# Moving the residual gates' sums, packing the keys' weights and taking turns with results in a two-layer attention trunk

## The chip, the cores and the metric

The kernel runs on one core of one Trainium2 chip. The metric is device time in microseconds of one execution. TensorE (PE) multiplies, VectorE (DVE), ScalarE (ACT) and GpSimd (POOL) work on tiles, and SyncE (SP) issues the transfers (DMAs). Each engine takes its own instructions strictly in order; between engines they wait on semaphores.

## The reference

Two layers of a trunk over 512 latent tokens (an 8 x 64 grid) and 256 context tokens, 1,024 channels. Each layer is one mixer with two branches that share an input projection:

```
mod = silu(c) @ w_ada + b_ada            # shift, scale, gate: 3 x 1024; for x and for ctx
h   = rmsnorm(x, norm_g) * (1 + scale) + shift
a_k, a_v, b_k, b_v, a_q, b_q, a_z, b_z, g_a, g_b = split(h @ w_in)
a   = neighbourhood attention(qknorm(a_q), qknorm(a_k), a_v) + all context keys    # 8 heads of 64
b   = grouped attention(rope(qknorm(b_q)), rope(qknorm(b_k)), b_v)                 # 8 query, 2 key heads
o   = sigmoid(g_a) * ((a * silu(a_z)) @ w_o_a) + sigmoid(g_b) * ((b * silu(b_z)) @ w_o_b)
x   = x + gate * (o @ w_out)
```

Layer 0 does this for the context too (which attends to the context alone); layer 1 updates the latent tokens only. The result is x. What the text calls the residual gate is the last third of `mod`.

## The kernel before

Tokens lie in tiles of 128: four latent, two of context. Activations are kept with channels on the partitions (`hx`, 8 blocks of 128 channels). Numbers are float32; each product of two matrices is made of three (`mm3`, lines 344 to 348): both sides are split into a high part (a cast on ACT) and a low part (a subtraction on DVE or POOL), and high x high, high x low and low x high are added up. A token projection of 512 columns (`tok_proj`, line 356) is thus 24 PE products of 128x512 for each token tile; a channel projection (`chan_proj`, line 363) is the same with the weights as the stationary side.

A layer goes through these stages: keys of branch A (`C_AK`, 512 columns), values of A (`C_AV`), queries of A (`C_AQ`), neighbourhood attention over 8 heads, keys and values of branch B (`C_BKV`, 256 columns), queries of B (`C_BQ`), grouped attention over 8 heads, the second output projection, and `w_out` with the residual. Inside the attention stages a list of pieces (`fill`: projections of the z paths and of the g gates, then `w_o_a`) is spread over the heads by `pipeline` (line 822), so that PE has products to do while softmax runs on the other engines. For head h, `scores_of(h)` makes four score tiles (PE), and for each the maximum (DVE), the exponential (ACT), the reciprocal and the scaling of the probabilities (DVE, or POOL for two of four). `values_of(h - 1)` transposes probabilities in groups of four 128x128 blocks (line 654), splits them (cast on ACT, line 657; subtraction on DVE, line 658) and multiplies them with the values.

Weights: `load_w` (line 308) loads one block of 128 channels at a time into one of three `raw` buffers, casts it on ACT into `whi` and subtracts into `wlo`; these are rings of 8 buffers in the pool `wp`, or, with `own`, rings of 8 in a pool of the stage. `load_w2` (line 323) loads two blocks of 256 columns into one 128x512 buffer and so does cast and subtraction for both at once. The queries of A and of B use `own`; the pool of B's stage (`bp`) reuses the memory of the neighbourhood attention's pool and can be written only when that memory comes free.

Sums for `mod`: `ada_steps` (line 200) yields steps. One loads a part of silu(c) to all partitions (`cb`); each of the others loads a 128x512 block of `w_ada` (`rawb`, two buffers, 256 KB) and makes a sum of products over its columns on DVE (line 222). The blocks 16 to 23 are those of the residual gate, two halves (h) each, and two vectors (latent and context) in layer 0, one in layer 1: 32 sums in layer 0, 16 in layer 1. They are made in grouped attention, `att["per"]` steps after each score tile (two in layer 0, one in layer 1), and are followed by `ada_gate`, which writes the gate to memory (`gd`) to be read before the residual. The blocks 0 to 15 of layer 1's `mod` are summed in layer 0: half 0 in the values' and queries' tiles of A, half 1 in the `w_out` stage.

Evacuation of key and query results: `head_rstd` (square on ACT, sum on DVE, two steps on POOL), multiply (DVE), for B the rotation (`rope_heads`, line 464: multiply with the cosines on DVE, with the sines on POOL, add on DVE), then transposes on PE. These are put off: `to_channels` appends them to `hp["late"]`, and `tok_proj` emits those that are more than `hp["lag"]` tiles old, chained to stand behind PE's last instruction (`after_products`, line 381). The lag is 2. In layer 0 the first projection is made for all six token tiles at once, in six PSUM banks, as the normalised input arrives; its six results are then evacuated one after the other (lines 595 to 600) before the values' tiles begin.

What is written in this order is then ordered by the framework, engine by engine, before the run: it places instructions by estimated times and by the emission order as priority. Buffers wait for their last reader.

Of the kernel before, what the change touches and what calls it, by code (L numbers as in the profile page):

```python
# [7 lines left out]
F32 = mybir.dt.float32  # L8
# [18 lines left out]
NP_GQ = (10, 10)  # L27
# [4 lines left out]
PRE_NA, PRE_GQ = 1, 2  # L32
XB, RX = 6, 2
# [14 lines left out]
def hybrid_kernel(es: ExitStack, tc, x, ctx, cvec, w_ada, w_ada0, small, gvec, w_in, w_o_a, w_o_b, w_out,  # L48
# [151 lines left out]
    def ada_steps(l, tiles, halves, nv, pool):  # L200
# [13 lines left out]
        def dot(h, i, v):  # L214
# [4 lines left out]
            ins = nc.cur_bb.bb.instructions  # L219
            before = next(j for j in reversed(ins) if j.engine == mybir.EngineType.DVE)  # L220
            n = len(ins)
            V.tensor_tensor_reduce(o, w, cb[h][:, v, :], 1.0, 0.0, ALU.mult, ALU.add, asum[:, i, h, v:v + 1])
            for j in nc.cur_bb.bb.instructions[n:]:
                if j.engine == mybir.EngineType.DVE:
                    tc.add_manual_dep(j, before.name, mybir.DependencyInfo(
                        mybir.DependencyClass.NoSync, mybir.DependencyReason.DATA), reason="program order")
# [81 lines left out]
    def load_w(src, col0, n, nk, lo_eng, k0=0, own=None):  # L308
# [3 lines left out]
        for k in range(k0, k0 + nk):  # L312
            raw = raw_tile()
            nc.sync.dma_start(raw[:, :n], src[128 * k:128 * k + 128, col0:col0 + n])
            hi = pool.tile([128, 512], F32R, tag="whi" + x, name=nm("whi"), bufs=8)
            S.copy(hi[:, :n], raw[:, :n])  # L316
            lo = pool.tile([128, 512], F32R, tag="wlo" + x, name=nm("wlo"), bufs=8)
# [63 lines left out]
    def after_products(fn):  # L381

        ins = nc.cur_bb.bb.instructions
        n, pe = len(ins), mybir.EngineType.PE
        last = next(i.name for i in ins[::-1] if i.engine == pe)
        fn()
        for i in nc.cur_bb.bb.instructions[n:]:
            if i.engine == pe:
# [4 lines left out]
    def turn_late(n):  # L393

        while len(hp["late"]) > n:
            after_products(hp["late"].pop(0))
# [67 lines left out]
    def rope_heads(npair, ps, rs, ta, tb, dst, t):  # L464
# [4 lines left out]
        r = hp["p"].tile([128, n], F32, tag=f"rr{npair}", name=nm("rr"), bufs=3)  # L469
# [11 lines left out]
    def layer(l, hx, nxt, mid):  # L481
# [5 lines left out]
        W = w_in[l]  # L487
        gq = gcol[:, 48 + 2 * l:49 + 2 * l]
# [93 lines left out]
        if first:  # L582
# [13 lines left out]
            for t in range(6):  # L596
                ev(t, pss[t])
            for fn in hp["late"]:
                fn()
            hp["late"] = []  # L600
            hp["lag"] = 2
            bg = ada_steps(1, range(16), (0,), 2, hp["p"])
        else:
            hp["p"] = bgp_es.enter_context(tc.tile_pool(name=f"cp{l}", bufs=1, reuse_waits="tile"))
            w = load_w(W, C_AK, 512, KT, mix_lo)
            for t in range(6):
                tok_proj(w, 512, a_hx, t, evac_na(kav, False, gk, 4))
            bg = []
# [3 lines left out]
        for t in range(6):  # L612
            tok_proj(w, 512, a_hx, t, evac_va(va))
            if t > 2:
# [20 lines left out]
        if True:  # L635
# [127 lines left out]
            def na_scores(h, q, kh, kl):  # L763
                load_bias(h)
                ps_ = []
                for i in range(4):
# [23 lines left out]
                    run(att["bg"], att["per"])  # L790
# [342 lines left out]
```

## Time and profile before

| | |
|---|---|
| median of three runs | 1167.61 us (1165.52 to 1169.21) |
| the profiled execution, its own time | 1166.55 us |
| its span, first to last instruction | 1164.8 us |
| mean granted clock of PE | 0.997 |
| PE busy | 1127.1 us of the span |
| DVE, ACT, POOL busy | 812.0, 574.3, 498.0 us |
| DMA | 134.05 MB, mean 115 GB/s |

Lines that begin with an engine, a line number and an operation are groups of instructions or single ones; out<-in are the program's tile names (`pst` the PSUM tile of transposes, `pss` of scores, `psv` of values, `psf` and `psx` of projections; `pth` and `ptl` the parts of the split probabilities; `rr` rotated keys or queries; `gah` and `gal` the gated result of branch A; `raw`, `whi`, `wlo` the weights; `rawb`, `cb` the operands of the sums for `mod`). The number in "L654" is the line of the kernel. PE's products overlap, and their ends are modelled, so a busy PE is not a PE at its peak; the time from one start to the next tells more. In a chain, "issue" is time in which an engine waited for nothing that the profile shows.

The stages by time, in us from the span's start: start-up and first projection to 75, values and queries of A to 150, neighbourhood attention to 310, keys and queries of B to 386, grouped attention to 565, closing projections to 700, and in layer 1 keys, values and queries of A to 782, neighbourhood attention to 897, keys and queries of B to 957, grouped attention to 1096, closing projections to the end.

### The profile page before, as it was taken

How to read it: one execution, taken by the hardware profiler on the slowest of the kernel's cores; microseconds unless marked ns; L12 is line 12 of the kernel's file. 1: busy time of each engine (PE TensorE's matmuls, PEld its weight loads, DVE VectorE, ACT ScalarE, POOL GpSimd, SP SyncE). 2: the span in 40 equal slices, each digit the busy share in tenths (PEclk: the TensorE clock that was granted, in tenths of full speed). 3: DMA queues.
4: the chain of work that ended last, by engine and by line, in shares of the span. 5: the costliest groups of instructions: out<-in, count | busy, mean ns of one | idle time of the engine just before them, and what ended most of it. 6: DMA issues, size and time to landing. Idle time of an engine off the chain costs nothing.

```text
span 1164.8 us, 17332 instructions
## 1 busy us (share of the span) xinstructions
PE 1127.1 (97%) x6078; PEld 948.9 (81%) x6078; DVE 812.0 (70%) x1512; ACT 574.3 (49%) x1175; POOL 498.0 (43%) x463
## 2 busy tenths in 40 slices
PE   5999999999999999999999999999999999999998
PEld 4688888988988888888788787888888878877686
DVE  4556588876364799798588755349877757898573
ACT  5452266665343555666431355337665445756531
POOL 3362354443275334353411227345544664645311
PEclk9999999999999999999999999999999999999999
DMA  9534212221351343461434423403322525452133
GB/s 372 200 110 136 71 46 65 84 83 63 111 164 47 115 134 100 81 259 37 139 133 123 151 71 92 126 25 107 104 74 66 171 90 182 142 176 91 37 132 95
DMA packets 88129, 134.05 MB, mean 115 GB/s; under 512 B 10757, under 2 KB 52713, under 8 KB 86377
## 3 DMA queue, kind: packets, MB, share of 16 engines
q1 hardware_dynamic: 88040, 132.94, 35.3%
q8 instruction: 48, 0.79, 0.3%
q14 instruction: 41, 0.33, 0.1%
HBM read 115.58 MB, written 17.32 MB: 114 GB/s over the span
## 4 chain that ended last, share of the span: by engine, by line
PE 72%; DVE 10%; POOL 6%; issue 4%; DMA 3%; ACT 2%; SPq 0%; ACTq 0%; POOLq 0%; DVEq 0%
PE psx L348 10%; PE psx L346 10%; PE psx L347 10%; PE psf L346 8%; PE psf L347 8%; PE psf L348 8%; PE pst L654 4%; PE pss L703 2%; PE pss L704 2%; PE pss L780 2%; POOL rsb L255 2%; DVE ptl L658 2%; DMA rawb<-in_w_ada_dram 1%; PE psv L948 1%; DVE mx L930 1%
## 5 line engine op out<-in xcount | busy, mean ns | idle before, releaser
L658 DVE TENSOR_TENSOR ptl<-pst,pth 128x512 fp32r<-128x512 f32 (+1 forms) x176 | 116.1, 671 | 41.0 <-ACT pth L657 40.0
L657 ACT CAST pth<-pst 128x512 fp32r<-128x512 f32 (+1 forms) x176 | 98.9, 576 | 91.7 <-PE pst L654 63.3
L346 PE MATMUL psf<-hx,whi 128*128 128x512 f32 (+1 forms) x368 | 139.4, 379 | 0.0
L347 PE MATMUL psf<-hx,whi 128*128 128x512 f32 (+1 forms) x368 | 138.3, 376 | 0.0
L348 PE MATMUL psf<-hx,wlo 128*128 128x512 f32 (+1 forms) x368 | 138.2, 375 | 0.0
L333 POOL TENSOR_TENSOR wlo<-raw,whi 128x512 fp32r<-128x512 f32 x64 | 91.0, 1425 | 109.9 <-ACT whi L331 96.5
L346 PE MATMUL psx<-whi,hx 128*128 128x512 f32 (+1 forms) x368 | 136.9, 373 | 0.0
L347 PE MATMUL psx<-wlo,hx 128*128 128x512 f32 (+1 forms) x368 | 136.2, 370 | 0.0
L348 PE MATMUL psx<-whi,hx 128*128 128x512 f32 (+1 forms) x368 | 133.8, 370 | 0.0
L319 POOL TENSOR_TENSOR wlo<-raw,whi 128x512 fp32r<-128x512 f32 (+1 forms) x52 | 67.4, 1296 | 149.6 <-ACT whi L316 132.0
L316 ACT CAST whi<-raw 128x512 fp32r<-128x512 f32 (+1 forms) x112 | 65.2, 592 | 112.6 <-PE psx L348 38.3
L331 ACT CAST whi<-raw 128x512 fp32r<-128x512 f32 x128 | 77.6, 621 | 53.2 <-DMA raw<-in_w_in_dram 39.6
L654 PE MATMUL pst<-ident,p 128*128 128x128 f32 x640 | 100.6, 273 | 1.7 <-DVE ptl L658 1.2
L654 PEld LDWEIGHTS pst<-ident,p 128*128 128x128 f32 x640 | 78.1, 141 | 13.7 <-DVE ptl L658 1.0
L644 POOL TENSOR_TENSOR p<-p,r 128x512 f32<-128x512 f32 (+1 forms) x64 | 85.7, 1339 | 5.2
L333 DVE TENSOR_TENSOR wlo<-raw,whi 128x512 fp32r<-128x512 f32 x64 | 62.7, 980 | 31.0 <-ACT whi L331 30.6
L319 DVE TENSOR_TENSOR wlo<-raw,whi 128x512 fp32r<-128x512 f32 (+1 forms) x60 | 48.2, 807 | 45.9 <-ACT whi L316 45.6
L643 POOL TENSOR_SCALAR r<-r 128x1 f32<-128x1 f32 x64 | 21.5, 336 | 137.1 <-DVE r L638 126.6
L346 PEld LDWEIGHTS psx<-whi,hx 128*128 128x128 f32 x368 | 69.8, 190 | 11.9 <-issue 0.8
L348 PEld LDWEIGHTS psf<-hx,wlo 128*128 128x128 f32 x368 | 69.4, 189 | 11.9
L348 PEld LDWEIGHTS psx<-whi,hx 128*128 128x128 f32 x368 | 69.6, 189 | 11.3
L346 PEld LDWEIGHTS psf<-hx,whi 128*128 128x128 f32 x368 | 69.5, 189 | 11.1 <-ACT zt L502 0.3
(239 smaller groups left out, 3065.8 us busy)
## 6 DMA issues: line engine op xcount, KB each, us to landing
raw<-in_w_in_dram SPq DMA_DIRECT2D x160, 256.0 KB, 2.9
rawb<-in_w_ada_dram SPq DMA_DIRECT2D x64, 256.0 KB, 2.7
gs<-zt SPq DMA_DIRECT2D x32, 256.0 KB, 2.4
raw<-in_w_out_dram SPq DMA_DIRECT2D x32, 256.0 KB, 2.8
tg<-gs SPq DMA_DIRECT2D x4, 1536.0 KB, 8.6
rawx<-in_w_ada_dram SPq DMA_DIRECT2D x4, 1024.0 KB, 6.4
rawy<-in_w_ada_dram SPq DMA_DIRECT2D x4, 1024.0 KB, 12.2
raw<-in_w_o_a_dram SPq DMA_DIRECT2D x16, 256.0 KB, 3.3
```

Source lines behind the costliest of these rows:

```text
L255: G.tensor_tensor(b[:, :w], a[:, :w], ehalf[:, :w], ALU.pow)
L316: S.copy(hi[:, :n], raw[:, :n])
L319: e.tensor_tensor(lo[:, :n], raw[:, :n], F(hi[:, :n]), ALU.subtract)
L331: S.copy(hi, raw)
L333: lo_eng(i).tensor_tensor(lo, raw, F(hi), ALU.subtract)
L346: T.matmul(ps, lhs[0], rhs[0], start=first, stop=False)
L347: T.matmul(ps, lhs[0], rhs[1], start=False, stop=False)
L348: T.matmul(ps, lhs[1], rhs[0], start=False, stop=last)
L644: G.tensor_tensor(p[:, c0:c1], p[:, c0:c1], r[:, i:i + 1].to_broadcast([128, c1 - c0]), ALU.mult)
L654: T.transpose(pt[:, c0:c0 + 128], src, ident)
L657: S.copy(hi[:, n0:n1], pt[:, n0:n1])
L658: V.tensor_tensor(lo[:, n0:n1], pt[:, n0:n1], F(hi[:, n0:n1]), ALU.subtract)
```

## The change

1. The residual gate's sums are yielded by `gate_steps(halves, pool)`. Layer 0 makes half 0 in the neighbourhood attention, one step after each score tile from head 4 on, and half 1 (followed by `ada_gate`) in grouped attention, one step after each score tile. Layer 1 makes both halves in the values' and queries' tiles of A, and none in grouped attention. Grouped attention of layer 1 has 11 buffers for probabilities instead of 10.
2. The weights of B's keys and values are loaded with `load_w2`. Those of B's queries are loaded before the keys' products, the first four blocks into `wp`, the other four into a ring of four in the stage's pool.
3. During B's keys the lag is 3 instead of 2, with a fourth buffer for rotated keys. The cosine and sine tables for the queries are made after the third key tile; before, they were made with those for the keys, ahead of all.
4. In layer 0, five results of the first projection are evacuated before the values' tiles, the sixth after the first of them; their transposes are put off with a lag of 4 that goes down to 2.

```diff
-NP_GQ = (10, 10)
+NP_GQ = (10, 11)
...
-    def load_w(src, col0, n, nk, lo_eng, k0=0, own=None):
+    def load_w(src, col0, n, nk, lo_eng, k0=0, own=None, bufs=8):
...
-        r = hp["p"].tile([128, n], F32, tag=f"rr{npair}", name=nm("rr"), bufs=3)
+        r = hp["p"].tile([128, n], F32, tag=f"rr{npair}", name=nm("rr"), bufs=4 if npair == 1 else 3)
...
+        nv = 2 if first else 1
+
+        def gate_steps(halves, pool):
+            return (ada_steps(l, range(16, 24), halves, nv, pool)
+                    + ([lambda: ada_gate(l, nv)] if 1 in halves else []))
...
-            for t in range(6):
+            for t in range(5):
                 ev(t, pss[t])
-            for fn in hp["late"]:
-                fn()
-            hp["late"] = []
-            hp["lag"] = 2
+            hp["lag"] = 4
             bg = ada_steps(1, range(16), (0,), 2, hp["p"])
         else:
...
-            bg = []
+            bg = gate_steps((0, 1), hp["p"])
+            run(bg, 1)
...
         for t in range(6):
             tok_proj(w, 512, a_hx, t, evac_va(va))
+            if first:
+                if t == 0:
+                    ev(5, pss[5])
+                hp["lag"] = max(2, hp["lag"] - (t > 0))
             if t > 2:
                 run(bg, per_bg)
...
-                    run(att["bg"], att["per"])
+                    run(att["bg"], 1)
...
-                att["bg"], att["per"] = bg, -(-len(bg) // 30)
                 prev = None
                 for h in range(8):
+                    att["bg"] = bg if h > 3 or pm["n"] == 1 else []
...
-            pipeline(fill, 9, na_first, values_of(za, na_values))
+            bg = gate_steps((0,), att["p"]) if first else []
+            pipeline(fill, 9, na_first, values_of(za, na_values), bg=bg)
...
-            cosn = hp["p"].tile([128, 512], F32, tag="sq", name=nm("cosn"), bufs=2)
+            cosn = hp["p"].tile([128, 512], F32, tag="cosn", name=nm("cosn"), bufs=1)
...
-            for i in range(2):
+
+            def make_tabs(i):
                 for j in range(2):
                     V.tensor_tensor(tabs[:, i, j], cosn[:, j],
                                     gbc[:, i, :].unsqueeze(1).to_broadcast([128, 4, 64]), ALU.mult)
+            make_tabs(1)
...
-            w = load_w(W, C_BKV, 256, KT, mix_lo)
+            bg = []
+            w = load_w2(W, C_BKV, KT, mix_lo)
+            w_q = load_w(W, C_BQ, 512, 4, bq_lo) + load_w(W, C_BQ, 512, 4, bq_lo, 4, hp["p"], 4)
+            hp["lag"] = 3
             for t in range(6):
                 tok_proj(w, 256, a_hx, t, evac_bkv)
+                if t == 2:
+                    behind(ON_DVE, lambda: make_tabs(0))
+                run(bg, 1)
+            hp["lag"] = 2
             qbv = big("qb").rearrange("p (j n) -> p j n", j=4)
-            w = load_w(W, C_BQ, 512, KT, bq_lo, own=hp["p"])
...
-            nv = 2 if first else 1
-            bg = ada_steps(l, range(16, 24), (0, 1), nv, att["p"]) + [lambda: ada_gate(l, nv)]
-            run(bg, 1)
+            bg = gate_steps((1,), att["p"]) if first else []
             pipeline(fill, 8, gq_first, values_of(zb, gq_values), early, bg)
```

`behind(engine, fn)` is `after_products` with the engine as a parameter; the sums use it with DVE, as they did before with the same code in place.

More of the change, by code (lines that the diff above doesn't have):

```diff
@@ L218, in dot @@
             o = w if v == nv - 1 else pool.tile([128, 512], BF16, tag="junk", name=nm("junk"), bufs=1)
[L219 to L226, printed above, removed]
+            behind(ON_DVE, lambda: V.tensor_tensor_reduce(o, w, cb[h][:, v, :], 1.0, 0.0, ALU.mult, ALU.add,
+                                                          asum[:, i, h, v:v + 1]))
         res = []
@@ L379, in hybrid_kernel, with behind @@
     hp = {"late": [], "lag": 0}
[L381 removed]
+    def behind(engine, fn):
         ins = nc.cur_bb.bb.instructions
[L384 to L385 removed]
+        n = len(ins)
+        last = next(i.name for i in ins[::-1] if i.engine == engine)
         fn()
         for i in nc.cur_bb.bb.instructions[n:]:
[L388 removed]
+            if i.engine == engine:
                 tc.add_manual_dep(i, last, mybir.DependencyInfo(
@@ L395, in turn_late @@
         while len(hp["late"]) > n:
-            after_products(hp["late"].pop(0))
+            behind(ON_PE, hp["late"].pop(0))
     def run(fill, n):
```

11 lines of the change are left out of this document (7 added, 4 removed).

## The prediction

> **What bounds the kernel now.** I read the page's busy shares first, then TensorE's (PE's) waits, then busy time by stage, then the chain and the timelines where PE stands still.
>
> ```profile
> PE 1127.1 (97%) x6078; PEld 948.9 (81%) x6078; DVE 812.0 (70%) x1512; ACT 574.3 (49%) x1175; POOL 498.0 (43%) x463
> ```
>
> PE is the bound: the sum of its idle is 38 us, and no edit here removes a product or a transpose (both built programs hold equally many). So the change can only win or lose PE's standing time. A busy share hides some of it, because ends are modelled; I therefore took PE's starts from the timeline. In dense stretches a 128x512 product starts 0.230 us after the one before, a 128x256 one 0.119, a transpose 0.108; what a step takes beyond this is loss. That gives 51 us in all: 14.6 before 70 us (start-up, not touched), 1.2 in 150 to 310 (layer 0's neighbourhood attention), 1.7 in 310 to 386 (its keys and queries of branch B), 4.3 in 386 to 475 and 4.0 in 475 to 565 (its grouped attention), 0.3 in 712 to 782 (layer 1's values and queries of A), 4.8 in 782 to 897 (layer 1's neighbourhood attention), 4.6 in 897 to 957, 2.3 in 957 to 1060, 8.8 in 1060 to 1096 (layer 1's branch B: projections, grouped attention, its end). Between 70 and 150 it is zero.
>
> ```profile
> PE pst L422 <- DVE rr L477: 4.1, 7, 1.4
> PE psv L948 <- DVE ptl L658: 2.0, 7, 0.5
> ```
>
> Outside start-up the named waits are those two: transposes of rotated keys or queries (L422), and value products behind the split in DVE (L658). By stage (columns: stretch, length, then PE, weight load, DVE, ACT, POOL busy):
>
> ```profile
> 220.00:310.00 90.00, 90.00 (x572) 80.68 (x571) 55.76 (x114) 48.81 (x112) 31.96 (x36) 1.00 0.19 63
> 385.00:475.00 90.00, 88.03 (x519) 75.98 (x517) 82.49 (x161) 49.23 (x107) 31.85 (x28) 1.00 0.36 115
> ...
> 712.00:782.00 70.00, 69.64 (x323) 57.21 (x323) 27.99 (x40) 28.34 (x48) 33.31 (x29) 1.00 0.28 84
> ...
> 957.00:1060.00 103.00, 101.63 (x520) 84.61 (x519) 85.04 (x153) 62.82 (x121) 50.80 (x43) 1.00 0.52 166
> 1060.00:1096.00 36.00, 32.16 (x172) 23.50 (x171) 27.54 (x46) 22.50 (x44) 16.78 (x16) 1.00 0.11 36
> ```
>
> DVE is at 92% where grouped attention carries the gate sums (L222) in layer 0 and at 83% in layer 1, but at 62% and 40% in the two stretches to which they go.
>
> **The change part by part**, against the profiled execution's 1166.55 us (span 1164.8); the median of the runs, 1167.61, is 1.1 above it.
>
> *Gate sums moved.* Layer 0 keeps 16 of its 32 sums in grouped attention, one step per score tile instead of two; 16 go to heads 4 to 7 of neighbourhood attention. All 16 of layer 1 go to its values' and queries' tiles.
>
> ```profile
> L222 DVE CUSTOM_DVE_ANT_0 rawb<-rawb,cb x64: 667/691/1889, 92.5 to 1030.4; 128x512 f32<-128x512 f32 x64
> ```
>
> In 385 to 475 its 32 sums took 27.7 us, 0.87 each; 16 fewer free 13.9 us of 82.5, so DVE falls to about 76%. Stretches at such a load lose little: 150 to 220, with DVE at 88% (61.3 of 70), lost 0.5. I take 1.7 of the 4.3 back; ends 0 (the losses are latencies) and 3.5. The 4.0 after 475 lies in a part whose order on PE is unchanged: 0.
>
> In layer 1 two of the last sums stand just ahead of a stall of 1.1 us:
>
> ```profile
> 1017.52 1.78 DVE L222 CUSTOM_DVE_ANT_0 rawb<-rawb,cb 128x512 f32<-128x512 f32 x1
> ...
> 1019.31 1.70 DVE L222 CUSTOM_DVE_ANT_0 rawb<-rawb,cb 128x512 f32<-128x512 f32 x1
> ```
> ```profile
> 1023.55 0.50 PE L703 MATMUL pss<-gk,qs 128*128 128x512 f32 x1 [0.91 <-ACT p L932]
> ```
>
> Two sums, 3.5 us, delay maximum and exponential, and the score product behind them waits. Gone: 1.5 of the 2.3 (ends 0 and 2.0). The 16 sums there take 14.7 us; with them gone, and an eleventh buffer for probabilities, the built order puts scores ahead. After the last output-projection piece of `w_o_a` that can fill a gap, the old order has 6 score tiles and 22 groups of four transposes left, the new one 1 and 16. In this end PE loses 8.8 us in 22 groups, 0.4 each. Six groups fewer are 2.4 us. One stall of 1.4 us (1078.4) comes from two exponentials of 0.90 on ACT ahead of a cast that PE needs; with five score tiles gone I take 1.1 of it. Sum 3.5; ends 0 (the groups meet a busy DVE elsewhere) and 6.
>
> What they cost where they go. Neighbourhood attention, layer 0: 55.8 us of DVE plus 16 at 0.87, 14, are 70 of 90, 78%; the stretch at 88% lost 0.5 in 70 us, so 0.6; I take 1.0, with -0.3 and +3.8 (the 385 to 475 rate, 4.3 in 90) as ends. Layer 1's values and queries: 28 plus 14 are 42 of 70. Its 16 weight loads (256 KB, 2.7 us to landing) and two vector loads now stand on SP's queue, and the write of the gate ahead of the first bias load; a load waits for the sum two before it, so SP can stand for a tile (5.5 us) before the next weights. Layer 0 does the same from 92 to 134 with 32 sums, and PE lost nothing there. 0.5; ends 0 and 3.
>
> A sum's cost is not one number: 97 of 112 took 0.69 us on average, 15 took 1.59, and POOL ran during 24% of the short ones' time, 80% of the long ones'. The Trainium skill (SBUF — State Buffer, Who interferes with whom) has the rule: a DVE instruction with two SBUF inputs contends with a GpSimd one that reads SBUF, and the later of the two is blocked; these rows agree, and it speaks against putting sums beside POOL's work.
>
> *Keys' weights packed, queries' weights earlier.* Eight loads, casts and splits of 128x256 become four of 128x512, in both layers; the casts are then 4 x 0.62 us. Half the queries' weights move ahead of the keys' products, into the slots that this frees; four, not eight, still wait for attention's memory to come free. That is the cause of layer 1's queue:
>
> ```profile
> 918.03 4.69 DMA raw<-in_w_in_dram
> ...
> 922.75 0.62 ACT whi L331
> ...
> 926.11 1.68 POOL rsb L255
> ...
> 949.49 1.76 DVE rr L477
> ```
>
> The first query tile ends on PE at 917.9, but ACT stands at weight casts until 923.9 before it squares it, so its transposes come to PE 1.4 us late (932.5), and the ones after it queue on POOL. In the new order one cast stands there, not two after a 2.5 us wait. From 918 the chain (square 0.6, sum 0.7, POOL 2.3, multiplies 1.4, POOL 1.3, add 0.7, issue) ends near 926.5, PE wants it at 931.
>
> *Rotated keys later.* A lag of three tiles gives one 2.9 us tile more before a key's transpose; the tables for queries (one pair of multiplies, 0.75 us) leave the start of the stage. Together I take back 3.7 of 4.6 in layer 1 (ends 0 and 4.4) and 0.8 of 1.7 in layer 0 (0 and 1.5). Price: the second weight chunk of the gates now needs the slots that the queries hold, so two casts and two POOL splits (1.3 each) stand among the last query tiles' chains; the new order also puts layer 1's third query transposes 33 products after the second ones instead of 20, 3.0 us more cover.
>
> *First projection.* Five results are copied at once and the sixth after the values' first tile, transposes spread over six tiles. PE lost nothing between 70 and 150, with DVE at 65%: 0, and the cover is six result banks; if it fails, one copy (0.7) shows.
>
> Sum: -1.7 -1.5 -3.5 +1.0 +0.5 -3.7 -0.8 = -9.7, so 1156.9; I say 1157.
>
> **Rivals.**
> *The end of layer 1 stays latency-bound.* For it: after 1080.7 no maximum and no exponential is left there, and PE still loses 4.1 us in eleven groups. Then the 3.5 stay: 1160.4.
> *Shared reads.* If all moved sums meet POOL, each takes 1.59: neighbourhood attention has 81 of 90 us on DVE and pays 3.8 instead of 1.0: 1159.7. Against it: POOL is busy 36% there, 35% where they came from. The page above would make it so only where POOL's reads come first.
> *The change moves the stalls.* The orders are fixed ahead of time; stalls freed in one place may reappear at the next instruction in line, as 4.8 us in layer 1's neighbourhood attention and 4.0 after 475 are untouched. Then some 2 us net remain: 1164.5.
> *Slower: the shared weight slots.* ACT is in order. If a cast of the second gate chunk waits for the queries' last tile, all behind it (square, copies of transposes) waits, and PE at those transposes. One tile of products, 5.5 us, in each layer, with the 4.5 of this stage not won: 1156.9 + 4.5 + 11 = 1172.4. It decides from about 4 us a layer on. Against: slots come free one by one as the last tile passes them, the first 0.7 us after it starts.
>
> **How the numbers follow.** Forecast 0.45 (own range 1152 to 1161), end latency 0.18, shared reads 0.12, moved stalls 0.13, slots 0.12. About 0.3% (3.5 us) is what a measurement of this kernel can tell from no change. The first three are faster, 0.75; moved stalls 0.13 is the same; slots 0.12 is slower. The range runs from 1151 (the good ends of half the terms) to 1167, leaving out most of the slots' case and little below.
>
> **What would show it.** Right: DVE near 78% in layer 0's grouped attention up to 475; no 1.4 us wait of L422's transposes in layer 1; the square of the first query tile within 1 us of its product; less than 5.5 us lost in the last 36 us before the closing projections. Wrong: PE waits inside layer 0's heads 4 to 7 for maxima; SP standing at gate loads while a weight is due; ACT standing at a weight cast among the query tiles.

## The result, and the profile after

| | before | after |
|---|---|---|
| median, us | 1166.57 (4 runs, 1165.51 to 1169.21) | 1156.08 (4 runs, 1154.84 to 1156.70) |
| profiled execution, its span | 1166.55, 1164.8 | 1154.84, 1153.1 |
| PE's mean granted clock | 0.997 | 0.998 |

The ratio is 0.9905, with an interval of 0.9885 to 0.9926: faster by 10.5 us. The forecast was 1157, from the likeliest case and the sum of its seven terms. The profiled execution of the changed kernel is the fastest of its four, 1.2 us under their median; the traces therefore differ by a little more than the medians do.

The page of the changed kernel, busy times and the chain that ended last by engine:

```profile
PE 1123.5 (97%) x6078; PEld 949.3 (82%) x6078; DVE 811.9 (70%) x1508; ACT 573.2 (50%) x1167; POOL 494.5 (43%) x459
...
PE 83%; DVE 7%; issue 3%; POOL 2%; ACT 2%; DMA 1%; ACTq 0%; POOLq 0%; DVEq 0%
```

The other engines' busy times are as before within 1%, as are the counts on PE. What differs is where the work stands: in the profile before, the same row of the chain began `PE 72%; DVE 10%; POOL 6%`. The chain that ended last now lies on PE for 83% of the span. PE's busy share, 97% in both, says nothing of this.

PE's waits in the last 36 us before the closing projections changed, and so did those in layer 1's keys and queries of B. After, from 940 to 1090 us (waiting instruction, what it waited for, us in total, times, longest):

```profile
PE psv L961 <- DVE ptl L661: 1.8, 2, 1.5
PE pst L657 <- DVE ptl L661: 0.9, 2, 0.4
```

The wait of the transposes (line 422 before, 417 after) for rotated keys and queries, 4.1 us before and the longest outside start-up, has no row at all now. The value products are still the ones that wait for the split in DVE.

Busy time by stretch, after (length, then PE, weight load, DVE, ACT, POOL): layer 0's neighbourhood attention from 219, its grouped attention from 386, layer 1's values and queries of A, its grouped attention, and its end.

```profile
219.00:311.00 92.00, 91.65 (x585) 82.08 (x585) 69.89 (x149) 50.27 (x113) 38.83 (x36) 1.00 0.29 88
386.00:475.00 89.00, 88.11 (x534) 77.40 (x533) 68.55 (x130) 50.29 (x107) 30.62 (x28) 1.00 0.28 87
711.00:781.00 70.00, 70.00 (x324) 57.74 (x324) 38.73 (x73) 27.41 (x47) 33.31 (x27) 1.00 0.52 142
...
949.00:1060.00 111.00, 110.70 (x576) 92.41 (x575) 89.08 (x137) 71.34 (x138) 52.33 (x48) 1.00 0.33 110
1060.00:1084.00 24.00, 21.23 (x114) 15.33 (x112) 16.23 (x24) 14.07 (x27) 11.87 (x11) 1.00 0.13 46
```

DVE fell to 77% where half of the sums left (386 to 475), rose to 76% and 55% where they went, and the end is 24 us long, not 36.

To compare kernels I took PE's loss in each stage as the prediction did: the time from one PE start to the next beyond 0.230, 0.119 and 0.108 us. Stages are bounded here by events, the first and last product of their kind, and not by the clock, so that a shift doesn't move work between them; "GQ" is grouped attention, "NA" neighbourhood attention, "w" the last piece of the output projection `w_o_a` that can fill a gap. One profiled execution each, us:

| stage | before | after | sums alone | weights alone | lag undone |
|---|---|---|---|---|---|
| start-up, A's projections, layer 0 | 14.3 | 14.6 | 15.0 | 15.0 | 14.4 |
| NA, layer 0 | 1.2 | 1.7 | 1.6 | 1.2 | 1.6 |
| B's keys and queries, layer 0 | 1.7 | 0.5 | 2.3 | 0.7 | 0.2 |
| GQ, layer 0, to the first `w_o_a` piece | 5.5 | 3.1 | 3.2 | 4.7 | 3.2 |
| GQ, layer 0, rest | 4.1 | 4.4 | 4.0 | 4.4 | 4.4 |
| closing, layer 0 | 2.2 | 1.4 | 2.1 | 1.4 | 2.0 |
| A's projections, layer 1 | 0.8 | 0.5 | 0.5 | 0.8 | 0.5 |
| NA, layer 1 | 4.8 | 4.8 | 4.8 | 4.8 | 4.9 |
| B's keys and queries, layer 1 | 4.6 | 0.2 | 4.1 | 0.1 | 0.9 |
| GQ, layer 1, to w | 2.3 | 1.6 | 1.7 | 2.4 | 1.5 |
| GQ, layer 1, its end | 8.7 | 6.1 | 6.1 | 8.7 | 6.0 |

The differences between before and after (with -0.8 in both for the closing part of layer 1) add up to -11.6 before rounding, -11.3 by the table's rounded figures; the spans differ by 11.7. So the whole gain is PE's standing time, in four places: the projections of B in both layers, the first part of layer 0's grouped attention, and the end of layer 1's. The first row runs from 13.8 to 18.0 and "closing, layer 0" from 1.3 to 2.2 over the kernels below without order by their edits; what changes only there I don't read. A stage that two kernels have alike loses the same in both: neighbourhood attention of layer 1 loses 4.8 or 4.9 in all twelve kernels, here and below, that leave it as it is, and the end is the same within 0.1 us in the five that have the sums moved and nothing else changed there, and in the five that have it as before.

### The profile page after: what moved, and what is told of

The parts are those of the page before. It is cut to its first block, busy times and chain, and to the rows that moved or that the text cites. A ratio compares the mean times of both kernels' runs of the same rounds, so it can differ in the third digit from the quotient of the medians.

```text
span 1153.1 us, 17284 instructions
## 1 busy us (share of the span) xinstructions
PE 1123.5 (97%) x6078; PEld 949.3 (82%) x6078; DVE 811.9 (70%) x1508; ACT 573.2 (50%) x1167; POOL 494.5 (43%) x459
## 4 chain that ended last, share of the span: by engine, by line
PE 83%; DVE 7%; issue 3%; POOL 2%; ACT 2%; DMA 1%; ACTq 0%; POOLq 0%; DVEq 0%
PE psx L341 12%; PE psx L343 12%; PE psx L342 12%; PE psf L341 9%; PE psf L342 9%; PE psf L343 9%; PE pst L657 4%; PE pss L706 2%; PE pss L707 2%; PE psv L961 2%; PE pss L783 1%; PE psv L960 1%; PE pst L417 1%; DVE wlo L328 1%; DVE ptl L661 1%
## 5 line engine op out<-in xcount | busy, mean ns | idle before, releaser
L661 DVE TENSOR_TENSOR ptl<-pst,pth 128x512 fp32r<-128x512 f32 (+1 forms) x176 | 116.0, 672 | 46.4 <-ACT pth L660 45.4
L328 POOL TENSOR_TENSOR wlo<-raw,whi 128x512 fp32r<-128x512 f32 x68 | 95.5, 1408 | 107.2 <-ACT whi L326 86.2
L314 POOL TENSOR_TENSOR wlo<-raw,whi 128x512 fp32r<-128x512 f32 x44 | 61.4, 1397 | 140.4 <-ACT whi L311 123.8
L326 ACT CAST whi<-raw 128x512 fp32r<-128x512 f32 x136 | 82.4, 621 | 55.6 <-DMA raw<-in_w_in_dram 39.6
L311 ACT CAST whi<-raw 128x512 fp32r<-128x512 f32 x96 | 58.7, 623 | 102.1 <-PE psx L343 38.6
L657 PE MATMUL pst<-ident,p 128*128 128x128 f32 x640 | 99.9, 272 | 1.4 <-DVE ptl L661 0.9
L328 DVE TENSOR_TENSOR wlo<-raw,whi 128x512 fp32r<-128x512 f32 x68 | 72.1, 1062 | 28.4 <-ACT whi L326 27.8
L657 PEld LDWEIGHTS pst<-ident,p 128*128 128x128 f32 x640 | 77.8, 140 | 13.3 <-DVE ptl L661 1.6
L341 PEld LDWEIGHTS psx<-whi,hx 128*128 128x128 f32 x368 | 69.7, 189 | 11.7 <-issue 0.8
L342 PEld LDWEIGHTS psx<-wlo,hx 128*128 128x128 f32 x368 | 69.7, 189 | 10.8
```

What stands on the lines that cost most here:

```text
L314: e.tensor_tensor(lo[:, :n], raw[:, :n], F(hi[:, :n]), ALU.subtract)
L326: S.copy(hi, raw)
L328: lo_eng(i).tensor_tensor(lo, raw, F(hi), ALU.subtract)
L341: T.matmul(ps, lhs[0], rhs[0], start=first, stop=False)
L342: T.matmul(ps, lhs[0], rhs[1], start=False, stop=False)
L657: T.transpose(pt[:, c0:c0 + 128], src, ident)
```

## The experiments

Twelve kernels, in three sets with runs of the kernel before on the same chip (medians 1166.72, 1166.19 and 1166.59). Ratios are to these; the changed kernel ran with a set of its own (1166.57). Theory: each part wins in its own stage, PE losing less because what it waits for is earlier, and the parts add up. Rivals: the end stays latency-bound; a moved sum only moves the stall; the gain of the weights is really the lag's, or the reverse.

**Each part alone.**

The sums alone, on the kernel before: `gate_steps` at all four places, and the eleventh buffer.

```diff
-NP_GQ = (10, 10)
+NP_GQ = (10, 11)
...
-            bg = ada_steps(l, range(16, 24), (0, 1), nv, att["p"]) + [lambda: ada_gate(l, nv)]
-            run(bg, 1)
+            bg = gate_steps((1,), att["p"]) if first else []
...
```

> The kernel before with the gate sums moved alone (and the eleventh buffer for probabilities in layer 1). My theory: the gains of the stages add up and each stage's belongs to one part. Then layer 0's grouped attention loses some 3 us on PE up to its first piece of w_o_a (5.5 before), the end of layer 1 some 6 (8.7 before), and the stage of B's keys and queries keeps its 4.6 in layer 1: about 1161, 5.5 under the kernel before. The rival, stalls that only move: freed time comes back at the next instruction in line, and the sums alone give less than 2 us.

Measured: 1161.60 us, ratio 0.9954 (0.9939 to 0.9969), 5.1 faster. By stage (column "sums alone"): the first part of layer 0's grouped attention -2.3, the end of layer 1 -2.7; the stages of B's projections change by +0.6 and -0.5 only.

The weights alone, on the kernel before: keys with `load_w2`, queries' weights ahead of the keys' products, half of them in `wp`. The lag and the tables stay.

```diff
-            w = load_w(W, C_BKV, 256, KT, mix_lo)
+            w = load_w2(W, C_BKV, KT, mix_lo)
+            w_q = load_w(W, C_BQ, 512, 4, bq_lo) + load_w(W, C_BQ, 512, 4, bq_lo, 4, hp["p"], 4)
...
-            w = load_w(W, C_BQ, 512, KT, bq_lo, own=hp["p"])
...
-                tok_proj(w, 512, a_hx, t, evac_bq)
+                tok_proj(w_q, 512, a_hx, t, evac_bq)
```

> The kernel before with the keys' weights packed and the queries' weights loaded ahead alone; the lag stays 2, the tables are made at the start. My theory: the weights are the cause of layer 1's late query transposes, so PE loses 1 us or less of 4.6 in layer 1's keys and queries of B and about 0.7 of 1.7 in layer 0's: about 1162, 4.5 under the kernel before. The rival: the lag is what frees PE, and the weights alone give 1 us or less. The other rival, slots shared between queries' and gates' weights: ACT stands at a weight cast among the query tiles, and the stage gets longer than before.

Measured: 1160.91 us, ratio 0.9948 (0.9932 to 0.9965), 5.8 faster. The loss in layer 1's keys and queries of B is 0.1 of 4.6: all of it goes without the lag. Layer 0's first part of grouped attention loses 0.8 less as well, which does not add to the sums' 2.3: the whole change has 2.4 there. In the five kernels that keep all 32 sums there (before and four of those here) this row runs from 4.7 to 5.5, so the 0.8 can't be put down to the weights.

The lag undone, on the changed kernel: both tables at the start of the stage, a lag of 2.

```diff
+            make_tabs(0)
             make_tabs(1)
...
-            hp["lag"] = 3
             for t in range(6):
                 tok_proj(w, 256, a_hx, t, evac_bkv)
-                if t == 2:
-                    behind(ON_DVE, lambda: make_tabs(0))
```

> The changed kernel with the lag back at 2 and both pairs of tables at the start. My theory: worth 0.5 us or less, so 1156 to 1157, with 0.2 to 1 us lost in layer 1's keys and queries of B. The rival, the lag as the cause: 3 to 4 us come back, about 1160.

Measured: 1155.90 us, ratio 0.9912 (0.9897 to 0.9927), the same as the whole change. In its trace layer 1's stage of B loses 0.9 where the changed kernel loses 0.2, and layer 0's 0.2 where that loses 0.5. With the weights in place the lag has 0.7 us left to win in one stage, and the total doesn't show it.

The first projection alone, on the kernel before:

```diff
-            for t in range(6):
+            for t in range(5):
                 ev(t, pss[t])
...
-            hp["lag"] = 2
+            hp["lag"] = 4
...
+            if first:
+                if t == 0:
+                    ev(5, pss[5])
+                hp["lag"] = max(2, hp["lag"] - (t > 0))
```

> The kernel before with the first projection's evacuation changed alone. My theory: PE lost nothing between 70 and 150 us before and loses nothing now, so no change of time within 1 us. The rival: the six banks are no cover, and a values tile waits for the sixth result, 1 to 3 us slower.

Measured over ten runs: 1166.75 us, ratio 1.0003 (0.9990 to 1.0015). No effect within 0.15%.

The four together: -5.1, -5.8, 0 and nothing measurable make -10.9; the whole change measured -10.5. The parts add up.

**The two halves of the weights.** Packing alone:

```diff
-            w = load_w(W, C_BKV, 256, KT, mix_lo)
+            w = load_w2(W, C_BKV, KT, mix_lo)
```

> The kernel before with the keys' weights packed and nothing else; the queries' weights still follow the keys' products into a ring of eight. My theory: the gain of layer 1's keys and queries of B (4.5 us) comes from ACT, which stood at gate weight casts ahead of the first query tile's square because eight query blocks waited for attention's memory and held the three raw buffers; packing alone leaves that queue, so 3 us or more are still lost there and the time is 1165 to 1166. The rival: eight small loads, casts and splits were the cost; packing gives most of the 5.8 us of the two together, about 1162.

Order alone, with the queries' weights ahead of the keys' products, all eight in the stage's pool:

```diff
             w = load_w(W, C_BKV, 256, KT, mix_lo)
+            w_q = load_w(W, C_BQ, 512, KT, bq_lo, own=hp["p"])
...
-            w = load_w(W, C_BQ, 512, KT, bq_lo, own=hp["p"])
...
-                tok_proj(w, 512, a_hx, t, evac_bq)
+                tok_proj(w_q, 512, a_hx, t, evac_bq)
```

> The kernel before with the loads of the queries' weights written ahead of the keys' products and nothing else: the keys' weights are not packed, so the ring of eight slots has no room, and all eight query blocks still wait for attention's memory. My theory: what counts is that half of the query blocks don't wait for that memory, for which packing makes the room; the order alone gives less than 1 us: 1165.5 to 1167, with 3.5 us or more still lost in layer 1's keys and queries of B. The rival: the place in the order, ahead of the keys' products, is the cause: 1 us or less lost there, about 1162.

Measured: 1164.39 (0.9988, 0.9978 to 0.9997) and 1164.42 (0.9988, 0.9976 to 1.0000), each over ten runs: 1.8 and 2.2 us between the medians, 1.4 by the ratios, the second of which isn't clear of no change. Together the halves stay under the 5.8 of both. In layer 1's stage of B the packing leaves 4.2 of 4.6, the order 1.9; in layer 0's the packing leaves 0.6 of 1.7 and the order 1.9. The square of the first query tile on ACT (`sq<-psf`, line 404 or 399) shows why. ACT's timeline (start, length, and in brackets the idle time before and what ended it) before:

```profile
922.75 1.25 ACT L331 CAST whi<-raw 128x512 fp32r<-128x512 f32 x2 [2.47 <-DMA raw<-in_w_in_dram]
923.90 0.60 ACT L404 ACTIVATE sq<-psf 128x512 f32<-128x512 f32 x1
```

ACT's timeline with packing alone:

```profile
919.72 1.27 ACT L331 CAST whi<-raw 128x512 fp32r<-128x512 f32 x2 [2.10 <-DMA raw<-in_w_in_dram]
920.89 0.59 ACT L404 ACTIVATE sq<-psf 128x512 f32<-128x512 f32 x1
```

ACT's timeline with the order alone:

```profile
918.37 0.62 ACT L331 CAST whi<-raw 128x512 fp32r<-128x512 f32 x1 [0.90 <-DMA raw<-in_w_in_dram]
...
919.80 0.62 ACT L331 CAST whi<-raw 128x512 fp32r<-128x512 f32 x1 [0.65 <-DMA raw<-in_w_in_dram]
920.33 0.59 ACT L404 ACTIVATE sq<-psf 128x512 f32<-128x512 f32 x1
```

with the weights alone, that is both:

```profile
914.26 0.62 ACT L331 CAST whi<-raw 128x512 fp32r<-128x512 f32 x1 [2.52 <-DMA raw<-in_w_in_dram]
...
916.08 0.60 ACT L404 ACTIVATE sq<-psf 128x512 f32<-128x512 f32 x1 [0.87 <-PE psf L348]
```

and in the whole change:

```profile
913.75 0.62 ACT L326 CAST whi<-raw 128x512 fp32r<-128x512 f32 x1 [3.48 <-DMA raw<-in_w_in_dram]
914.59 0.61 ACT L399 ACTIVATE sq<-psf 128x512 f32<-128x512 f32 x1
```

From the tile's end on PE to its square it is 6.0 us before, 5.7 with packing, 3.8 with order, 0.3 with both and 1.2 in the whole change. The cast that waits for its load is there in every one of them; what differs is whether it comes before or after the tile is ready. With both, ACT stands 2.5 us for the load too, but is through that cast 0.9 us before the tile ends (at 915.8), and the square waits for PE and for no cast. Neither half alone gets that far: the last casts ahead of the square still wait for a load (2.10 us with packing, 0.65 with order) and start 4.5 and 3.3 us after the tile's end. "Both" has one thing more than the two halves, four weight blocks in `wp` which need not wait for attention's memory; its share wasn't tried by itself. The transposes of this first tile followed their rotation by 0.2 us before (932.3 to 932.5), so PE had been waiting for them; in the changed kernel they come 4.0 us after it (922.7 to 926.7).

**The end of layer 1.** The eleventh buffer undone, on the changed kernel:

```diff
-NP_GQ = (10, 11)
+NP_GQ = (10, 10)
```

> The changed kernel with 10 buffers for probabilities in layer 1's grouped attention instead of 11. In its built order 18 groups of transposes and 4 score tiles come after the last piece that can fill a gap (16 and 1 in the changed kernel, 22 and 6 in the kernel before). My theory: what the end loses follows these counts, so some 7.3 us are lost there instead of 6.1, and the time is 1157 to 1157.5. The rival: the absence of the sums makes the whole gain, and the eleventh buffer is worth nothing; 6.1 lost, 1156. The other rival: the buffer makes all of it, 8.7 lost, 1158.5.

Measured: 1156.89 us, ratio 0.9921 (0.9904 to 0.9937); not told apart from the changed kernel by time. By stage the end loses 7.8 and not 6.1, and the part ahead of it 0.7 and not 1.6. So of the end's 2.7 the sums' leaving makes 0.9 and the buffer the rest; but the buffer costs 0.9 ahead of the end, where the sums' leaving had won 1.6. Over both parts the sums' leaving makes 2.5 of 3.3 and the buffer 0.8.

With ten buffers the stall before the change, `PE psv L947 <- ACT pth L657: 1.2, 1, 1.2`, is still there, behind the same two exponentials of 0.90 on ACT, though no sum is left in the stage. PE's wait from 1060 to 1087:

```profile
PE psv L960 <- ACT pth L660: 1.2, 1, 1.2
```

With eleven it is gone, and there is one of 1.53 us for the split in DVE instead (line 961, above).

Then the amount of filling. The list of pieces spread over nine heads' time and not eight, in layer 1:

```diff
-            pipeline(fill, 8, gq_first, values_of(zb, gq_values), early, bg)
+            pipeline(fill, 8 if first else 9, gq_first, values_of(zb, gq_values), early, bg)
```

> The changed kernel with the filling of layer 1's grouped attention spread over nine parts, not eight. In its built order 20 groups and 3 score tiles come after the last piece that can fill a gap, against 16 and 1. By 0.38 us a group the end loses 7.6 instead of 6.1, and what comes before 0.7 to 1.6: 1156.5 to 1158. If spreading helps, the stages before gain more than 1.5 us.

Two chunks of the g gates' projections in layer 1's neighbourhood attention, or four, where there are three (the rest goes to grouped attention):

```diff
-GATES = (3, 3)
+GATES = (3, 2)
```

> The changed kernel with one of layer 1's chunks of the g gates moved from neighbourhood attention to grouped attention as filling (2 chunks in the first instead of 3). In its built order 12 groups and no score tile come after the last piece that can fill a gap. If the end's loss goes by the groups, 0.37 us each, it falls from 6.1 to 4.5; neighbourhood attention with 11 us less to fill would lose some 1 us more than its 4.8: 1155 to 1156. If neighbourhood attention was already short of filling, it loses 3 us or more beyond and the time is 1158 or more.

```diff
-GATES = (3, 3)
+GATES = (3, 4)
```

> The changed kernel with four chunks of layer 1's g gates in neighbourhood attention instead of three, the opposite of the run with two. There neighbourhood attention lost 10.4 us with 11 us of filling less; if it goes on that way, it loses 2 to 4 us now, and grouped attention, with 26 groups and 7 score tiles after the last filling, 9 or more in its end: 1157 to 1160. If the end doesn't follow the groups, 1154 to 1155.

Measured: 1158.40 us (ratio 0.9934, 0.9916 to 0.9951), 1162.74 (ten runs; 0.9974, 0.9964 to 0.9984) and 1163.67 (ten runs; 0.9981, 0.9970 to 0.9992). The last two are slower than the changed kernel. The first is 2.3 us above it, but its interval overlaps the changed kernel's (0.9885 to 0.9926); its trace has 3.6 us more loss in layer 1's grouped attention. What the built order leaves after w, and what PE loses there:

| kernel | groups of four transposes left | score tiles left | loss in the end, us | GQ ahead of it | NA, layer 1 |
|---|---|---|---|---|---|
| two chunks | 12 | 0 | 3.6 | 5.2 | 10.4 |
| changed kernel | 16 | 1 | 6.1 | 1.6 | 4.8 |
| ten buffers | 18 | 4 | 7.8 | 0.7 | 4.9 |
| spread over nine | 20 | 3 | 8.2 | 3.1 | 4.9 |
| before | 22 | 6 | 8.7 | 2.3 | 4.8 |
| four chunks | 26 | 7 | 14.4 | 2.8 | 3.6 |

A group left is 0.38 to 0.43 us lost from 16 to 22 groups, and 0.30 at 12; at 26, 0.55. So the end does follow what is left there; groups and score tiles grow together over these kernels, and the table doesn't separate them. With two chunks the end wins 2.5 us more, as the theory has it, but the neighbourhood attention that lost its filling pays 5.6 and the grouped attention 3.6. PE's waits there with two chunks, from 785 to 892:

```profile
PE psv L809 <- DVE ho L670: 2.7, 3, 1.8
PE pst L655 <- DVE ptl L661: 1.2, 2, 0.9
```

and in the end with four chunks, from 1050 to 1096:

```profile
PE psv L961 <- DVE ptl L661: 4.9, 7, 1.8
PE pst L657 <- DVE ptl L661: 1.0, 2, 0.6
```

Three chunks stand between two stages that both lose when a chunk goes to the other.

**Where the sums cost least.** All 32 of layer 0 in heads 4 to 7 of neighbourhood attention, two after each score tile, on the changed kernel:

```diff
-            bg = gate_steps((0,), att["p"]) if first else []
+            bg = gate_steps((0, 1), att["p"]) if first else []
...
-                    run(att["bg"], 1)
+                    run(att["bg"], 2)
...
-            bg = gate_steps((1,), att["p"]) if first else []
+            bg = []
```

> The changed kernel with all 32 gate sums of layer 0 in heads 4 to 7 of its neighbourhood attention, two after each score tile, and none in grouped attention. It doubles the cost that the change put there. My theory: DVE has room there (it would go from 78% to about 93%), so PE's loss in that stage goes from 1.65 to 2.5 or 3.5 us and the grouped attention's first part from 3.1 to 1.5 or 2: no change within 1.5 us. The rival, shared reads: the sums meet POOL, DVE is full and PE loses 5 us or more in neighbourhood attention, 1159 or more.

Half 1 in the tiles of B's keys (one each) and queries (two each):

```diff
-            bg = []
+            bg = gate_steps((1,), hp["p"]) if first else []
             w = load_w2(W, C_BKV, KT, mix_lo)
...
-            bg = gate_steps((1,), att["p"]) if first else []
+            run(bg, len(bg))
```

> The changed kernel with layer 0's second half of the gate sums moved on, from grouped attention to the tiles of B's keys (one step each) and queries (two steps each), where DVE is busy for 52% of the stage. By DVE's load this should cost little there and free grouped attention of all sums. But with no sums there at all, grouped attention's first part still lost 2.6 us of 3.1, and POOL, with which the sums share reads, is at 56% in B's stage: I expect no gain, 0 to 1 us slower (1156 to 1157.5). If load is what counts, 1 us or more faster.

Measured: 1158.76 us (ratio 0.9945, 0.9928 to 0.9962) and 1158.96 (0.9947, 0.9928 to 0.9966), both above the changed kernel by nearly 3 us, with intervals that don't meet its own. Stretches 219 to 315 and 390 to 478 of the first:

```profile
219.00:315.00 96.00, 94.02 (x594) 83.23 (x594) 81.28 (x184) 51.21 (x116) 40.71 (x37) 1.00 0.44 116
390.00:478.00 88.00, 87.33 (x535) 77.23 (x534) 60.57 (x102) 53.09 (x112) 29.24 (x29) 1.00 0.21 68
```

and its waits on PE in the first of the two, where the changed kernel has only `PE pst L655 <- DVE ptl L661: 0.4, 1, 0.4`:

```profile
PE pst L655 <- DVE ptl L661: 1.3, 2, 0.8
PE psv L814 <- DVE ptl L661: 0.5, 1, 0.5
```

The first 16 sums cost neighbourhood attention 0.5 us, the next 16 2.9 (1.2, 1.7, 4.5 us lost, with DVE busy 73%, 81% and 87% of the time from 150 to 310). With no sum left, grouped attention still loses 2.6 of the 3.1 that it loses with 16. With half 1 in B's projections those lose 2.7, 2.2 more, and grouped attention, also free of sums, 4.5. So its loss does not follow the number of sums alone. PE's timelines show what else sets it: two stalls, one at the third score tile, which waits for the first exponential, and one at the first product of `w_o_a`. With all sums in neighbourhood attention, from 385 to 496:

```profile
PE psf L341 <- ACT zt L502: 1.1, 1, 1.1
PE pss L706 <- ACT p L945: 0.7, 1, 0.7
```

From start to start they cost 1.2 and 0.8 us, and they are as long before, with 32 sums, and after, with 16. What is left of the loss beside these 2.1 does go by the sums: 3.4 before, with 32 of them (2.7 to 3.4 in the other kernels that keep all), 1.0 with 16, 0.5 with none. With half 1 in B's projections the second score tile waits too, 0.6 us, and the third 2.0: ahead of the first maximum DVE makes a weight's split whose cast came late. The rest is 0.6 there.

Not tried: the lag alone on the kernel before; it was tested only by undoing it on the changed kernel.

## Why the prediction was right, point by point

| term | foreseen, us | measured | shown by |
|---|---|---|---|
| layer 0's grouped attention, 386 to 475 (measured to the first `w_o_a` piece) | -1.7 | -2.4 | sums alone: -2.3 |
| layer 1's grouped attention, to 1060 | -1.5 | -0.7 | sums alone: -0.7 |
| its end | -3.5 | -2.7 | sums alone: -2.7 |
| sums in layer 0's neighbourhood attention | +1.0 | +0.5 | sums alone: +0.5 |
| sums in layer 1's values and queries of A | +0.5 | -0.3 | sums alone: -0.3 |
| B's keys and queries, layer 1 | -3.7 | -4.4 | weights alone: -4.5 |
| B's keys and queries, layer 0 | -0.8 | -1.2 | weights alone: -1.0 |
| first projection | 0 | not told from its spread | alone: 0.0 in time |

Every sign but one small one was right, and no term is off by more than 0.8 us; five came out better than foreseen by more than 0.3, in sum by 3.1, and two worse, by 1.6 (both in layer 1's grouped attention). Together the terms are -11.2 where -9.7 was the sum. The rest of the -11.6 lies in stages that vary without the edits. That the median came within 1 us of the forecast is in part luck: the errors of the terms offset each other by half.

*The bound.* That only PE's standing time is to be won held: the spans differ by 11.7 and PE's starts by 11.6.

*Sums out of layer 0's grouped attention.* The mechanism held, DVE fell to 77% (76% foreseen) and PE lost 2.4 less. The term was taken at half of its upper end, too low: beside the two stalls that don't change, the loss fell from 3.4 to 1.0. The unchanged part behind it (4.0 foreseen as untouched) is 4.4.

*Sums out of layer 1's.* 1.5 was mis-sized: 0.7. The 1.1 us stall that followed two sums is gone, as the step had it. With ten buffers the stretch loses 0.7, 1.6 less than before, which is what was foreseen; the eleventh buffer, put into the same change, gives 0.9 of it back here and wins it in the end.

*The end of layer 1.* Six groups at 0.4, 2.4 of the 2.7, fit the table above. The other 1.1, for the stall behind two exponentials on ACT, was the mis-sized step. The row of a value product that waits for ACT's cast is gone from this stretch, but as long a stall stands in the new one, at a value product that waits for the split in DVE. From PE's timeline after, then DVE's and POOL's:

```profile
1064.90 0.50 PE L961 MATMUL psv<-ptl,vb 128*128 128x512 f32 x1 [1.53 <-DVE ptl L661]
```
```profile
1062.50 1.75 DVE L328 TENSOR_TENSOR wlo<-raw,whi 128x512 fp32r<-128x512 f32 x1
1064.17 1.28 DVE L661 TENSOR_TENSOR ptl<-pst,pth 128x512 fp32r<-128x512 f32 x2
```
```profile
1062.23 1.47 POOL L647 TENSOR_TENSOR p<-p,r 128x768 f32<-128x768 f32 x1
```

The split that PE waits for stands behind a weight's split of 1.75 us, which began while POOL scaled a probability tile and ended 0.55 us after POOL did; about half of these splits (L328 on DVE, 68 in all) take 0.67 to 0.69. So the new stall is another one, on another engine, and it came with the eleventh buffer (the old one is there with ten). The third rival, stalls that only move, holds here in so far as one went and one came. The first rival, an end bound by latency that gives nothing back, fell: of its 3.5 us 2.7 came. "Less than 5.5 us lost" failed: it is 6.1.

*Sums where they went.* 0.5 in neighbourhood attention, half of what was taken; PE's one named wait there (0.4 us) is for a split and not for a maximum, which would have been the sign of a wrong price. The row that the step leaned on, 0.5 us lost in a stretch with DVE at 88%, was right for this dose; as a rule it fails, since at 87% with 32 sums the same stage loses 4.5. The share of DVE's time doesn't price a sum; that what stands next in DVE's line behind it does is my reading and was not tested. In layer 1's values and queries the fear for SP's queue was empty: the loss there is smaller than before (0.5 against 0.8).

*Shared reads.* The rival asked for all the moved sums to be long. In neighbourhood attention 4 of 16 took over 1 us, mean 0.86; in layer 1's values and queries 1 of 16, mean 0.75; over the kernel 11 of 112, where 15 were long before. It did not decide.

*The weights of B.* The named cause held and is shown: the square of the first query tile moved from 6.0 us behind its product to 1.2 (0.3 with the weights alone; "within 1 us", the sign foreseen, was missed by a little), and the transposes' wait of 1.4 us is gone. It was foreseen that the chain ends near 926.5 with PE wanting it at 931; rotation was done at 922.7 and PE came at 926.7, the cover 4.0 where 4.5 were expected. The size was taken too low: the sum left 0.9 of the 4.6 us as the price of the casts of the gates' chunk among the query tiles, and only 0.2 was left. From ACT's timeline after, they do stand there,

```profile
926.25 0.60 ACT L399 ACTIVATE sq<-psx 128x512 f32<-128x512 f32 x1
926.74 1.13 ACT L326 CAST whi<-raw 128x512 fp32r<-128x512 f32 x2
```

but behind the square of the third query tile, not ahead of it, and the first tile's transposes come 4.0 us after their rotation. So the slower rival, the shared weight slots, has its two casts and no price: loss in the stage 0.2 us in layer 1 and 0.5 in layer 0, where it needed 4 in each.

*The lag.* The prediction gave weights and lag one term together. The runs separate them: the weights make nearly all of it, the lag 0.7 us in one stage and nothing that the total shows.

*What the expectations of the experiments got wrong.* The order of the loads alone was to leave at least 3.5 us in layer 1's stage of B; it left 1.9, as the earlier order also brought the casts forward: the last one ahead of the square starts at 919.8, the last two of before at 922.8. All sums in neighbourhood attention were to change nothing beyond 1.5 us; they cost 2.7. Half of the sums in B's projections was to cost 1 us at most; it cost 2.9. Filling spread over nine was to leave 0.7 to 1.6 us lost ahead of the end; it left 3.1. Packing alone came out 0.6 us faster than its range. And the chunks of the g gates were priced too low: with two, neighbourhood attention was to lose some 1 us more and lost 5.6, and the 3.6 in grouped attention ahead of the end wasn't foreseen; with four, the end was to lose 9 us or more and lost 14.4, more for each group than with 22. The kernels are 6.7 and 7.6 us slower than the changed one.

## What to carry to other kernels

Where PE is 97% busy, measure what is left from its start-to-start times, stage by stage, and price an edit there: terms of 1 to 4 us, each read so, added up to within 1.5 us here. On an in-order engine whatever queues behind a weight cast waits for that cast's load, so a load is due when its cast would be in the way, not when the product needs the weight; look for the first small step of a long chain (here a square of 0.6 us) behind a cast that waits for a load. Spread optional work thinly: here 16 sums cost a stage 0.5 us and 16 more in it 2.9.

## What the runs showed that was not expected

*A sum is long beside wide work of POOL, not beside any.* Before, 97 of 112 sums took 0.69 us and 15 took 1.59. In the changed kernel 11 took over 1 us. Every one of them starts while POOL runs a two-operand instruction over 512 columns (eight times the subtraction of a weight block), and every one ends 0.55 to 0.56 us after that instruction does, whatever its own length (1.09 to 1.78 us). One of them in DVE's timeline after:

```profile
103.35 1.34 DVE L220 CUSTOM_DVE_ANT_0 junk<-rawb,cb 128x512 bf16<-128x512 f32 x1 [0.26 <-DMA rawb<-in_w_ada_dram]
```

and POOL's timeline at the same time:

```profile
102.85 1.29 POOL L328 TENSOR_TENSOR wlo<-raw,whi 128x512 fp32r<-128x512 f32 x1 [2.87 <-ACT whi L326]
```

POOL ended at 104.14 and the sum at 104.69. So a sum that starts second ends when POOL's instruction lets it, not after its own 0.69 us. It is so in all fourteen kernels: of their 1,568 sums 179 took over 1 us, and every one of these began beside such a wide two-operand instruction of POOL and ended 0.54 to 0.56 us after it. But of the 16 sums set into B's projections none was long (mean 0.68 us), though POOL was at work for 60% of their time. From that kernel, DVE's timeline:

```profile
344.42 0.68 DVE L220 CUSTOM_DVE_ANT_0 rawb<-rawb,cb 128x512 f32<-128x512 f32 x1
```

and POOL's:

```profile
343.38 1.92 POOL L250 TENSOR_TENSOR rsb<-rsa,ehalf 128x8 f32<-128x8 f32 x1
```

POOL's instruction runs from 1.04 us before the sum to 0.2 us after it, works on 8 columns, and costs it nothing. In all fourteen kernels 54 sums began during such a narrow one (128x8, two operands) with more than 0.16 us of it left; none took over 1 us. (A sum that starts with 0.13 us of a wide instruction left takes 0.67, one with 0.28 left 0.83: 0.55 after its end again.) The Trainium skill (SBUF — State Buffer, Who interferes with whom) says that a DVE instruction with two SBUF inputs contends with a GpSimd one that reads SBUF, and, in its Summary: rules for kernel authors, that the second one to issue blocks until the first finishes. The first pair agrees, with the 0.55 us beside it; the second pair differs from that wording, and the measurement decides: to price such a sum one asks what POOL's instruction is, not only whether POOL runs. The wide and the narrow instruction differ in operation as well as in width (the narrow one is a power), and which of the two counts was not separated; the profile's spans on POOL are rough.

*Grouped attention of layer 0 loses 2.6 to 4.5 us with no sums in it,* 3.1 with 16 and 5.5 with 32. Two stalls, 2.1 us together and as long with the sums as without, are the larger part of what is left; only half 1 in B's projections lengthens one of them. The loss beside them goes by the sums: 3.4 us with 32, 1.0 with 16, 0.5 with none.
